# Dense weight loads traced two uses ahead in the second half of a mixer, with the early expert loads queued behind them

## The chip, the cores and the metric

The kernel runs on one core of a Trainium2 chip. The metric is the device time of one execution in microseconds; the runs of the kernel before gave a median of 1898.48 us (1895.02 to 1900.64, three runs).

## The reference, cut to what matters

The network takes 256 tokens of width 1024 through one block of a first kind and two layers of a second kind. Only the second kind matters here. Each of its layers is a mixer followed by a mixture of experts:

```python
proj = jnp.einsum('bsd,dc->bsc', h, w_in)
qa, ka, va, qw, kw, vw, gates = jnp.split(proj, SPLITS, axis=-1)
oa = dilated_mixture(qa, ka, va);  ya = oa @ w_branch_a
ob = banded_attention(qw, kw, vw); yb = ob @ w_branch_b
g = sigmoid(gates + b_gate)
merged = g[:, :, 0] * ya + g[:, :, 1] * yb
x = x + merged @ w_out
...
gate, idx = lax.top_k(softmax(h @ w_router).T, cap)      # 32 tokens for each of 16 experts
ye = (silu(xe @ w_gate) * (xe @ w_up)) @ w_down          # xe = h[idx]
```

All weights are float32. The 16 experts of a layer have 192 MB of weights, the mixer some 32 MB.

## The kernel before, in words

Tokens lie on the free axis and features on the partitions, so a product with a weight matrix is a row of dense tiles. A weight chunk is 128 x 2048 float32, 1 MB, and is called a dense load: `load` (L116) takes a tile of the pool `ring`, which has three slots (`RING`, L54), and issues the DMA on SyncE's queue (L118). `split_w` (L121) then cuts each half of the chunk in a high and a low part, ScalarE writing the high part (L124, a cast) and VectorE the low part (L125, a subtraction). The result `ws` has four slots (`NSPLIT`). `mm3` (L129 to L132) does three matmuls with each 128x128 block. A ring slot is free again when both halves of its chunk are split; a `ws` slot when TensorE has used it, and when a POOL copy that reads it (below) is done.

`mixer` (second layer kind) has two halves. In the first the projections and both attentions are computed. The second begins after `att.close()`, which ends the pool of the attention's tiles: eight gate chunks (`gate(0)` to `gate(3)`, two chunks each, L922), five chunks of the branch matrices `w_br2` (L941), each chunk serving 16 blocks of the loop over `i` and `k`, and four chunks of `w_out2` in `out_tiles` (L684). In the order of use the 17 chunks are: gate 0 to 3, branch 0, branch 1, gate 4, gate 5, branch 2, gate 6, gate 7, branch 3, branch 4, out 0 to 3. Branch 0 ends before the loop's block 16, but the second half of branch 1 is first split after gates 4 and 5. At the end of every `i` a `merge` (L260) follows on VectorE and ScalarE; every gate chunk is followed by `over_rms` (L213, VectorE) and a tanh (L927, ScalarE).

The experts' weights stream through `Experts` (L1008). It has 23 places of 1 MB before any place comes free again: one `q`, four `a0`, six `a1` (in the memory that the attention gives back), `Ha` and `Hb` (the mixer's input, free after gate 7), one `b`, the three ring slots, the four `ws` slots and two more. Loads into `q` and `a0` are made in the mixer's first half. The six into `a1` come from `pace`, which is called after each gate chunk and at each branch chunk and loads one chunk as long as fewer than 11 are there. A paced load first has a one-column copy on GpSimd (L1040), which reads the low part of the newest split (`turn[0]`) and writes the place: so it can't start before that split, and the split's `ws` slot can't be reused before the copy.

The order of instructions on each engine is written by a planner: it simulates the program in time with its own costs, and gives each engine the ready instruction that was traced first. So the gate chunks, which don't need the attention's result, are run between the attention's instructions. On the chip each engine runs its list in order, SyncE's DMA issues too. As far as the trace's semaphores show, a tile gets the slot that comes free first. `tc.issue_after(x)` makes the planner put the DMAs traced in its block behind `x` on the same queue.

Of the kernel before, what the change touches and what calls it, by code (L numbers as in the profile page):

```python
# [53 lines left out]
RING, NA0, NA, NB, NSPLIT = 3, 4, 6, 1, 4  # L54
# [7 lines left out]
def tile_net(ctx: ExitStack, tc: tile.TileContext, a, out):  # L62
    nc = tc.nc
# [4 lines left out]
    sp = ctx.enter_context(tc.tile_pool(name="split", bufs=NSPLIT))  # L68
# [42 lines left out]
        return ps.rearrange("p (n t) -> p n t", n=2)  # L111


    turn = [None]

    def load(src):  # L116
        w = ring.tile([P, CH], F32, name="w", tag="w")
        nc.sync.dma_start(w, src)  # L118
        return w

    def split_w(sp, w, hf):  # L121
        ws = sp.tile([P, 2, 1024], F32R, name="ws", tag="ws")
        s = w[:, hf * 1024 : hf * 1024 + 1024]
        nc.scalar.copy(ws[:, 0], s)  # L124
        nc.vector.tensor_tensor(ws[:, 1], s, ws[:, 0].bitcast(F32), op=ALU.subtract)  # L125
        turn[0] = ws[:, 1]
        return ws[:, 0], ws[:, 1]
# [10 lines left out]
    def dense_pair(ps, w, sp, h, begun=None):  # L138

        for n in range(2):  # L140
            wh, wl = begun if begun and n == 0 else split_w(sp, w, n)
            dense_tile(ps[:, n, :], wh, wl, h)
# [18 lines left out]
    def act_pair():  # L161
        return tuple(hp.tile([P, KT, T], F32R, name=f"H{c}", tag=f"H{c}") for c in "ab")
# [113 lines left out]
    def first_block():  # L276
        with ExitStack() as es:
# [19 lines left out]
            h = act_pair()  # L297
# [223 lines left out]
            with tc.tile_pool(name="b1g", bufs=2, side="right", reuse_waits="tile") as gp:  # L521
# [69 lines left out]
                M = qp.tile([P, 2, KT, T], F32R, name="M", tag="Qa")  # L591
                for i in range(8):
                    w = load(a["w_br"][i])
                    pA, pB = psd(), psd()
                    outs = [pA[:, 0:T]] * 8 + [pA[:, T:]] * 4 + [pB[:, 0:T]] * 4
                    for hf in range(2):
                        wh, wl = split_w(sp, w, hf)
                        for kk in range(8):
                            k = hf * 8 + kk
# [3 lines left out]
                h = act_pair()  # L603
                acc = new_acc()
                for j in range(4):
                    for k, ps in out_tiles(a["w_out1"][j], j, sp, M, psd):
                        nc.vector.tensor_tensor(x[:, k, :], ps, x[:, k, :], op=ALU.add)
                        square_in(acc, x[:, k, :], k == 0)
                        feed(h, k, vec("norm2_g", k))


            with tc.tile_pool(name="b1f", bufs=2) as tp:
# [5 lines left out]
                for j in range(DFF_T):  # L618
                    ps = pairs(psd())
# [12 lines left out]
                h = act_pair()  # L632
# [6 lines left out]
                blk = 0  # L639
                for c in range(11):  # L640
                    w = load(a["w_down1"][c])
                    for hf in range(2):
                        wh, wl = split_w(sp, w, hf)
                        for kk in range(8):
                            n, k = divmod(blk, DFF_T)
                            if k == 0:
                                ps = psd()
# [33 lines left out]

        return h, stats

    def out_tiles(src, j, sp, M, psd):  # L684

        w = load(src)
        for n in range(2):
            ps = psd()
            wh, wl = split_w(sp, w, n)
            dense_tile(ps[:, :T], wh, wl, (M[:, 0], M[:, 1]))  # L690
            yield 2 * j + n, ps[:, :T]


    def mixer(l, h, stats, w0=None):

        with ExitStack() as es:
# [31 lines left out]
            w1 = a["w_in2"]  # L728
# [74 lines left out]
            for j, pair in enumerate(WIN_PAIRS):  # L803
# [30 lines left out]
                for c in range(2):  # L834
                    for t in range(2):
                        i = 2 * c + t
# [26 lines left out]
            for j in range(2):  # L863
                pts = []
                for c in range(2):
                    s = 2 * j + c
                    b = slice(64 * c, 64 * c + 64)
                    pt = tp.tile([P, 2, 4, P], F32, name="pd", tag="zw")
                    pts.append(pt)
                    for t in range(2):  # L870
                        tk = slice(t * P, t * P + P)
                        z = tp.tile([P, 512], F32, name="zd", tag="pt", bufs=3)
                        ps = pss()
                        parts = ((s, slice(0, T), slice(0, T)), (4 + s, slice(256, 384), tk), (8 + s, slice(384, 512), tk))
                        score(ps[:, :T], qa0[:, j, c, tk], ka0[:, j, c], kl0[:, j, c])
                        for n, o, kr in parts[1:]:
                            i = n // 2 - 2
# [35 lines left out]
            M = qp.tile([P, 2, KT, T], F32R, name="M", tag="Qa")  # L913
            blk = 0
            tgs = []

            def gate(j):
                tg = yp.tile([P, 2, 2, T], F32, name="tg", tag="tg", bufs=2)
                tgs.append(tg)
                for i in range(2):  # L920
                    ps = pairs(psd())
                    dense_pair(ps, load(w1[l, 15 + 2 * j + i]), sp, h)  # L922
                    xl.pace()
                    over_rms(tg[:, i], ps, rms)
                    for n in range(2):
                        c = 8 * i + 2 * j + n
                        nc.scalar.activation(  # L927
                            tg[:, i, n, :], tg[:, i, n, :], AF.Tanh, bias=hb[:, c : c + 1], scale=0.5
                        )

            gate(0)
            for i in range(8):
                if i % 2 == 0 and i < 6:
                    gate(i // 2 + 1)
                if i == 5:

                    xl.prefetch(2, True)
                ps = psd()
                for k in range(10):
                    if blk % 16 == 0:  # L940
                        w = load(a["w_br2"][l, blk // 16])  # L941
                        xl.pace()
                    if blk % 8 == 0:
                        wh, wl = split_w(sp, w, blk // 8 % 2)
                    b = blk % 8 * P
                    mm3(ps[:, 0:T] if k < 2 else ps[:, T:], cols(wh, b, P), cols(wl, b, P),
                        Y[:, 0, k, :], Y[:, 1, k, :], k in (0, 2), k in (1, 9))
                    blk += 1
                merge(M, i, [tgs[i // 2][:, b, i % 2, :] for b in range(2)], [ps[:, 0:T], ps[:, T:]])
# [7 lines left out]
            at = PV["router"][0] + 256 * l  # L957
            pl = pss()
            for j in range(4):
                for k, ps in out_tiles(a["w_out2"][l, j], j, sp, M, psd):  # L960
                    gain = vec("norm_ffn", 8 * l + k)
                    if k < KT - 1:
                        nc.vector.tensor_tensor(x[:, k, :], ps, x[:, k, :], op=ALU.add)
                        nc.vector.tensor_scalar(xg[:, k, :], x[:, k, :], gain, None, op0=ALU.mult)
                        square_in(acc, x[:, k, :], k == 0)
                    else:
                        nc.vector.tensor_scalar(xg[:, k, :], x[:, k, :], gain, None, op0=ALU.mult)
                        nc.vector.scalar_tensor_tensor(xg[:, k, :], ps, gain, xg[:, k, :], op0=ALU.mult, op1=ALU.add)
                        nc.vector.tensor_tensor(x[:, k, :], ps, x[:, k, :], op=ALU.add)
                        sq7 = cp.tile([P, T], F32, name="sq7", tag="sq", bufs=2)  # L970
                        nc.scalar.activation(sq7, x[:, k, :], AF.Square)
                if j == 2:

                    nc.scalar.activation(cp.tile([P, 1], F32, name="far1", tag="far1"), acc[:, 0:1], AF.Sqrt)
                if j % 2 == 1:
                    for k in range(2 * j - 2, 2 * j + 2):
                        o = 32 * (k % 4)
                        nc.tensor.matmul(
                            pl[o : o + 32, :T], pv[:, at + 32 * k : at + 32 * k + 32], xg[:, k, :],
                            start=j == 1, stop=j == 3,  # L980
                        )
# [26 lines left out]
    class Experts:  # L1008


        def __init__(self, l):
            self.l, self.r2a, self.r2b, self.at, self.dma = l, [], None, 0, None
            self.have, self.n = [], 0

            self.cycle = ["q"] + ["a0"] * NA0 + ["a1"] * NA + ["Ha", "Hb"] + ["b"] * NB + ["r"] * RING + ["s"] * NSPLIT
            self.places = self.cycle + ["x", "x"]

        def load(self, paced=False):
            i = len(self.have)
            end = i >= NCHUNK - sum(cn for _, cn in ENDS) * KT // 512  # L1020
            while True:
                where = self.places.pop(0)
                if not self.places:
                    self.places = list(self.cycle)

                if not (end and where in ("Ha", "Hb")):
                    break
            if where == "x":
                t = self.extra.pop(0).rearrange("p a d -> p (a d)")
            elif where == "s":  # L1030
                t = sp.tile([P, 2, 1024], F32, name="we", tag="ws").rearrange("p a d -> p (a d)")
            else:
                pool, tag = {
                    "q": (qp, "Qb"), "a0": (self.r2a[0], "w2"), "a1": (self.r2a[-1], "w2"), "b": (self.r2b, "w3"),
                    "r": (ring, "w"), "Ha": (hp, "Ha"), "Hb": (hp, "Hb"),
                }[where]
                t = pool.tile([P, CH], F32, name="we", tag=tag)
            if paced:

                nc.gpsimd.tensor_copy(t[:, 0:1], turn[0][:, 0:1].bitcast(F32))  # L1040
            src = a["w_exp"][self.l, i]

            for c0, cn in ((0, 1024), (1024, 1024)) if i == NCHUNK - 1 else ((0, CH),):
                with tc.issue_after(self.dma.ins) if end else nullcontext():
                    self.dma = nc.sync.dma_start(t[:, c0 : c0 + cn], src[:, c0 : c0 + cn])
            self.have.append(t)

# [3 lines left out]

        def pace(self):

            if len(self.have) < 1 + NA0 + NA:
                self.load(True)

        def take(self):
            while len(self.have) <= self.n:
                self.load()
            self.n += 1  # L1060
            return self.have[self.n - 1]
# [404 lines left out]
```

## Time and profile before

| | |
|---|---|
| median of the runs | 1898.48 us |
| the profiled execution | 1898.55 us, its span 1896.8 us |
| TensorE, matmuls | 1600.4 us busy, 84% of the span |
| VectorE / ScalarE / GpSimd | 43% / 33% / 2% |
| DMA | 562.49 MB, 297 GB/s over the span |
| mean granted clock | 0.888 |

The first block runs from 0 to some 500 us. Then come the first layer's mixer (to 745 us), its router and experts (to some 1190 us), the second layer's mixer (to 1442 us) and its experts. Busy shares over the whole span mix stages with different limits: TensorE is the busy engine in the mixers, and the DMA engines are it in the experts' stages, at some 420 GB/s.

### The profile page before, as it was taken

To read this page: it belongs to the slowest core of one execution; us is meant where nothing else is said; L and a number is where in the kernel's file an instruction comes from. 1 tells how busy PE (TensorE), PEld (TensorE's weight loads), DVE (VectorE), ACT (ScalarE), POOL (GpSimd) and SP (SyncE) were. 2 spreads that over 40 slices of the span, in tenths; PEclk is the share of its full clock that TensorE was granted. 3 is DMA by queue.
4 is the path that set the end of the run, shared out by engine and by line. 5 is a ranking of instruction groups with operands and counts; after the bars stand their busy time and mean duration, and the time that the engine had idled before them with its cause. 6 is when DMAs were issued, how large, how long until landed. Compare 5 with 4: busy or idle time off the path is not lost.

```text
span 1896.8 us, 27588 instructions
## 1 busy us (share of the span) xinstructions
PE 1600.4 (84%) x11434; PEld 1081.8 (57%) x11434; DVE 823.2 (43%) x1481; ACT 629.2 (33%) x1130; POOL 46.3 (2%) x72
## 2 busy tenths in 40 slices
PE   8999999999999988876767666999898866766665
PEld 7899999999998987220111102888896311101101
DVE  7688787996687556100000001687464100000001
ACT  5567646666566443100000001566443100000001
POOL 0100000000011000000000000010000000000000
PEclk9999999999999999887777768999999887867768
DMA  6454554554553367999999999832577999999998
GB/s 248 167 190 167 178 178 179 187 190 178 217 223 112 147 267 275 397 419 420 420 420 419 420 420 418 332 129 102 222 266 277 418 420 419 419 420 419 420 421 321
DMA packets 83829, 562.49 MB, mean 297 GB/s; under 512 B 9452, under 2 KB 14456, under 8 KB 16888
## 3 DMA queue, kind: packets, MB, share of 16 engines
q1 hardware_dynamic: 83544, 560.20, 74.7%
q8 instruction: 90, 1.47, 0.3%
q10 hardware_dynamic: 160, 0.52, 0.1%
q14 instruction: 35, 0.29, 0.0%
HBM read 558.84 MB, written 1.85 MB: 296 GB/s over the span
## 4 chain that ended last, share of the span: by engine, by line
PE 54%; DMA 43%; DVE 2%; ACT 1%; issue 0%; SPq 0%; ACTq 0%; DVEq 0%
DMA we<-in_w_exp_dram 42%; PE ps_d L130 14%; PE ps_d L131 14%; PE ps_d L132 14%; PE ps_t L257 1%; PE ps_g L1172 1%; PE ps_v L846 1%; DMA w<-in_w_in_dram 1%; PE ps_u L1172 1%; PE ps_s L772 1%; PE ps_s L878 1%; PE ps_s L773 0%; PE ps_s L374 0%; PE ps_t L1187 0%; PE ps_v L896 0%
## 5 line engine op out<-in xcount | busy, mean ns | idle before, releaser
L130 PE MATMUL ps_d<-Ha,ws 128*128 128x256 f32 x1408 | 404.9, 288 | 14.7 <-ACT Ha L177 7.9
L132 PE MATMUL ps_d<-Ha,ws 128*128 128x256 f32 x1408 | 404.9, 288 | 5.0 <-DVE ws L125 4.9
L131 PE MATMUL ps_d<-Hb,ws 128*128 128x256 f32 x1408 | 403.6, 287 | 0.7 <-DVE Hb L178 0.7
L125 DVE TENSOR_TENSOR ws<-w,ws 128x1024 fp32r<-128x1024 f32 x282 | 342.6, 1221 | 119.7 <-ACT ws L124 117.0
L124 ACT CAST ws<-w 128x1024 fp32r<-128x1024 f32 x282 | 293.3, 1047 | 256.0 <-PE ps_d L132 223.3
L130 PEld LDWEIGHTS ps_d<-Ha,ws 128*128 128x128 f32 x1408 | 273.0, 194 | 18.4 <-ACT Ha L177 7.9
L132 PEld LDWEIGHTS ps_d<-Ha,ws 128*128 128x128 f32 x1408 | 273.0, 194 | 8.3 <-DVE ws L125 6.1
L131 PEld LDWEIGHTS ps_d<-Hb,ws 128*128 128x128 f32 x1408 | 272.9, 194 | 3.5 <-issue 1.2
L1172 PE MATMUL ps_u<-we,W 128*32 128x512 f32 x992 | 187.8, 836 | 90.4 <-DMA we<-in_w_exp_dram 90.3
L1172 PE MATMUL ps_g<-we,W 128*32 128x512 f32 x1024 | 175.9, 789 | 71.9 <-DMA we<-in_w_exp_dram 71.8
L1172 PE MATMUL ps_e<-we,W 128*32 128x512 f32 (+1 forms) x1152 | 162.6, 669 | 64.2 <-DMA we<-in_w_exp_dram 64.1
L1172 PEld LDWEIGHTS ps_u<-we,W 128*32 128x32 f32 x992 | 25.4, 125 | 239.2 <-DMA we<-in_w_exp_dram 223.1
L1172 PEld LDWEIGHTS ps_g<-we,W 128*32 128x32 f32 x1024 | 26.5, 123 | 205.7 <-DMA we<-in_w_exp_dram 165.3
L1246 ACT ACTIVATE W<-ps_g 128x512 f32<-128x512 f32 x16 | 9.6, 597 | 381.4 <-PE ps_g L1172 381.4
L1172 PEld LDWEIGHTS ps_e<-we,W 128*32 128x32 f32 x1152 | 29.4, 120 | 163.6 <-DMA we<-in_w_exp_dram 121.1
L1248 DVE SCALAR_TENSOR_TENSOR W<-W,ps_u 128x512 f32<-128x512 f32 x16 | 11.0, 688 | 247.1 <-PE ps_u L1172 247.1
L1201 DVE COPY W<-ps_e 128x512 f32<-128x512 f32 (+1 forms) x18 | 11.4, 632 | 221.5 <-PE ps_e L1172 221.5
L1247 DVE SCALAR_TENSOR_TENSOR W<-W,ps_g 128x512 f32<-128x512 f32 x16 | 11.0, 688 | 208.1 <-ACT W L1246 208.1
L1253 ACT COPY W<-ps_t 128x512 f32<-128x512 f32 x16 | 9.4, 586 | 275.9 <-PE ps_t L1252 275.9
L130 PE MATMUL ps_d<-Y,ws 128*128 128x256 f32 x288 | 81.4, 283 | 0.0
L132 PE MATMUL ps_d<-Y,ws 128*128 128x256 f32 x288 | 81.4, 283 | 0.0
L131 PE MATMUL ps_d<-Y,ws 128*128 128x256 f32 x288 | 81.4, 282 | 0.0
(327 smaller groups left out, 2371.9 us busy)
## 6 DMA issues: line engine op xcount, KB each, us to landing
we<-in_w_exp_dram SPq DMA_DIRECT2D x378, 1024.0 KB, 19.9
w<-in_w_in_dram SPq DMA_DIRECT2D x46, 1024.0 KB, 4.9
w<-in_w_up_dram SPq DMA_DIRECT2D x22, 1024.0 KB, 4.8
w<-in_w_br_dram SPq DMA_DIRECT2D x18, 1024.0 KB, 4.9
w<-in_w_gate_dram SPq DMA_DIRECT2D x12, 1024.0 KB, 4.9
w<-in_w_out_dram SPq DMA_DIRECT2D x12, 1024.0 KB, 4.9
w<-in_w_down_dram SPq DMA_DIRECT2D x11, 1024.0 KB, 4.9
w<-in_w_rnn_dram SPq DMA_DIRECT2D x8, 1024.0 KB, 4.8
```

The lines of the kernel that those rows point to most:

```text
L124: nc.scalar.copy(ws[:, 0], s)
L125: nc.vector.tensor_tensor(ws[:, 1], s, ws[:, 0].bitcast(F32), op=ALU.subtract)
L130: nc.tensor.matmul(ps, wh, xh, start=first, stop=False)
L131: nc.tensor.matmul(ps, wh, xl, start=False, stop=False)
L132: nc.tensor.matmul(ps, wl, xh, start=False, stop=last)
L257: nc.tensor.transpose(ps[:, i * P : i * P + P], b, ident)
L772: nc.tensor.matmul(ps, q, kh, start=True, stop=False)
L846: nc.tensor.matmul(po[64 * c : 64 * c + 64, :T], vw[:, k, kvh * 64 : kvh * 64 + 64], pts[c][:, k * T : k * T + T], start=k == 0, stop=k == 1,)
L878: nc.tensor.matmul(ps[:, o], qa[b, i, tk], ka[b, i, kr], start=True, stop=True)
L1172: nc.tensor.matmul(b[32 * e : 32 * e + 32, :cn], lhs[:, k, 32 * e : 32 * e + 32], cols(w, ((k - k0) * 4 + e) * cn, cn), start=k == 0, stop ...
L1201: nc.vector.tensor_copy(ye[:, s], E[:, :cn])
L1247: nc.vector.scalar_tensor_tensor(th, th, 1.0, G[n], op0=ALU.add, op1=ALU.mult)
```

## The change

Three things are changed. `line_up` takes the list of the 17 chunks in the order of use and gives a function `take`; each `take` first traces loads until three are traced and not yet taken, and hands out the oldest. So a load is traced two uses ahead of its own use; before it was traced at its use. `Experts.load` puts each paced load behind `turn[1]`, the dense load that was traced last. And the first four calls of `pace` in a layer load nothing (`self.wait = 4`), so the `a1` loads are traced at branch 0, branch 1, gate 4, gate 5, branch 2 and gate 6; before at gates 0 to 3, branch 0 and branch 1. `out_tiles` gets the tile instead of the source; for the first block this changes nothing.

```diff
     def load(src):
         w = ring.tile([P, CH], F32, name="w", tag="w")
-        nc.sync.dma_start(w, src)
+        turn[1] = nc.sync.dma_start(w, src)
         return w
+    def line_up(srcs):
+        srcs, ws = list(srcs), []
+        def take():
+            while srcs and len(ws) < RING:
+                ws.append(load(srcs.pop(0)))
+            return ws.pop(0)
+        return take
...
-                    dense_pair(ps, load(w1[l, 15 + 2 * j + i]), sp, h)
+                    dense_pair(ps, take(), sp, h)
...
+            order = [w1[l, 15], w1[l, 16]]
+            for i in range(8):
+                if i % 2 == 0 and i < 6:
+                    order += [w1[l, 17 + i], w1[l, 18 + i]]
+                order += [a["w_br2"][l, b // 16] for b in range(10 * i, 10 * i + 10) if b % 16 == 0]
+            take = line_up(order + [a["w_out2"][l, j] for j in range(4)])
...
-                        w = load(a["w_br2"][l, blk // 16])
+                        w = take()
                         xl.pace()
...
-                for k, ps in out_tiles(a["w_out2"][l, j], j, sp, M, psd):
+                for k, ps in out_tiles(take(), j, sp, M, psd):
...
-            self.have, self.n = [], 0
+            self.have, self.n, self.wait = [], 0, 4
...
-                with tc.issue_after(self.dma.ins) if end else nullcontext():
+                behind = self.dma if end else turn[1] if paced else None
+                with tc.issue_after(behind.ins) if behind else nullcontext():
...
         def pace(self):
-            if len(self.have) < 1 + NA0 + NA:
+            self.wait -= 1
+            if self.wait < 0 and len(self.have) < 1 + NA0 + NA:
                 self.load(True)
```

## Rows read from the trace of the kernel before

**Rows 1.** Page, part 4: shares of the chain that ended last, by engine.

```profile
PE 54%; DMA 43%; DVE 2%; ACT 1%; issue 0%; SPq 0%; ACTq 0%; DVEq 0%
```

**Rows 2.** Chain of waits, 655 to 800 us: start us, us, what, xcount.

```profile
744.45 0.83 PE ps_v L987 x6
...
757.59 3.52 PE ps_g L1172 x16
...
783.38 19.87 DMA we<-in_w_exp_dram
```

**Rows 3.** Timeline of PE around its two gaps, first layer [idle before <-releaser].

```profile
669.11 0.38 PE L132 MATMUL ps_d<-Ha,ws 128*128 128x256 f32 x1 [2.20 <-DVE ws L125]
...
677.53 0.39 PE L130 MATMUL ps_d<-Ha,ws 128*128 128x256 f32 x1 [2.66 <-ACT ws L124]
```

**Rows 4.** The same two gaps in the second layer.

```profile
1365.17 0.58 PE L132 MATMUL ps_d<-Ha,ws 128*128 128x256 f32 x1 [2.20 <-DVE ws L125]
1375.06 0.39 PE L130 MATMUL ps_d<-Ha,ws 128*128 128x256 f32 x1 [2.66 <-ACT ws L124]
```

**Rows 5.** Timeline of SP's DMA issues, 640 to 700 us, adjacent ones merged.

```profile
643.16 11.00 SPq L1045 DMA_DIRECT2D we<-in_w_exp_dram  x3
655.74 0.33 SPq L118 DMA_DIRECT2D w<-in_w_in_dram  x1
656.91 1.46 SPq L1045 DMA_DIRECT2D we<-in_w_exp_dram  x2
658.48 0.39 SPq L118 DMA_DIRECT2D w<-in_w_in_dram  x1
...
670.22 0.33 SPq L118 DMA_DIRECT2D w<-in_w_br_dram  x1
```

**Rows 6.** L118's loads, issue to landing: 570 to 625 us, then the one at 658.48.

```profile
DMA to landing us min/median/max: 4.8/4.9/5.0
...
DMA to landing us min/median/max: 13.4/13.4/13.4
```

**Rows 7.** Timeline of DVE, then of ACT, from 663 us.

```profile
666.71 0.42 DVE L265 SCALAR_TENSOR_TENSOR m<-tg,ps_d 128x256 f32<-128x256 f32 x1 [1.41 <-PE ps_d L132]
667.84 2.35 DVE L125 TENSOR_TENSOR ws<-w,ws 128x1024 fp32r<-128x1024 f32 x2
...
664.75 1.98 ACT L124 CAST ws<-w 128x1024 fp32r<-128x1024 f32 x2
675.64 0.91 ACT L927 ACTIVATE tg<-tg,hb 128x256 f32<-128x256 f32 x2 [7.27 <-DVE tg L213]
676.45 2.93 ACT L124 CAST ws<-w 128x1024 fp32r<-128x1024 f32 x3
```

**Rows 8.** Windows: stretch, us, busy us (xcount) by engine, PEclk, DMA share, GB/s.

```profile
679.01:682.42 3.41, 3.41 (x18) 3.41 (x17) 3.13 (x3) 1.42 (x2) 0.00 (x0) 0.50 0.46 108
682.42:685.83 3.41, 3.41 (x31) 3.41 (x29) 0.00 (x0) 0.95 (x1) 0.00 (x0) 1.00 1.02 425
1365.17:1368.50 3.33, 3.33 (x15) 3.33 (x16) 1.42 (x2) 0.00 (x0) 0.00 (x0) 0.50 1.02 406
```

**Rows 9.** Windows of the attention's end, the stretch behind it, and up to the experts.

```profile
620.00:652.50 32.50, 32.50 (x238) 28.26 (x236) 17.91 (x48) 14.71 (x30) 0.18 (x1) 1.00 0.27 98
652.50:666.60 14.10, 14.10 (x119) 14.09 (x119) 7.95 (x11) 8.17 (x12) 3.68 (x5) 1.00 0.87 350
700.00:757.50 57.50, 50.59 (x399) 46.85 (x397) 35.63 (x78) 22.99 (x36) 0.31 (x2) 0.94 0.74 286
```

**Rows 10.** Timeline of POOL, 640 to 654 us: copies before the a1 loads.

```profile
640.57 0.18 POOL L1040 COPY we<-ws 128x1 f32<-128x1 f32 x1 [35.61 <-PE ps_d L132]
653.14 0.30 POOL L1040 COPY we<-ws 128x1 f32<-128x1 f32 x2 [12.39 <-ACT Y L157]
```

**Rows 11.** Waits of SP's queue over the whole span: total us, times, longest us.

```profile
SPq L118 <- DVE ws L125: 414.4, 72, 12.0
```

**Rows 12.** Windows for line L130 alone (one of three dense lines): PE busy (xcount).

```profile
635.64:652.50 16.86, 7.34 (x25) 4.75 (x25) 1.00 0.34 125
```

More of the change, by code (lines that the diff above doesn't have):

```diff
@@ L111, in pairs @@
         return ps.rearrange("p (n t) -> p n t", n=2)
-    turn = [None]
+    turn = [None, None]
     def load(src):
         w = ring.tile([P, CH], F32, name="w", tag="w")
-        nc.sync.dma_start(w, src)
+        turn[1] = nc.sync.dma_start(w, src)
         return w
+    def line_up(srcs):
[5 more added lines that the diff above has]
+        return take
     def split_w(sp, w, hf):
@@ L605, in first_block @@
                 for j in range(4):
-                    for k, ps in out_tiles(a["w_out1"][j], j, sp, M, psd):
+                    for k, ps in out_tiles(load(a["w_out1"][j]), j, sp, M, psd):
                         nc.vector.tensor_tensor(x[:, k, :], ps, x[:, k, :], op=ALU.add)
@@ L682, in first_block, with out_tiles @@
         return h, stats
-    def out_tiles(src, j, sp, M, psd):
-        w = load(src)
+    def out_tiles(w, j, sp, M, psd):
         for n in range(2):
```

## The prediction

> **What bounds the kernel now.** I read four views. The page's chain of what ended last says that TensorE (54%) and DMA (43%) set the end, and nothing else does [rows 1]. In order of time the chain is TensorE up to the end of the mixer (744.45) and the router, the experts' first matmuls at 757.59, and from 783.38 one expert load after the other [rows 2]. So a mixer is bound by TensorE and an experts' stage by its stream, which can't run ahead: all 23 places are taken before the experts begin, and the next load waits for a place that they free. What the second half of a mixer gains or loses therefore moves everything behind it by as much, in both layers.
>
> Inside that half the reader is to see that TensorE is busy without a break, 32.50 of 32.50 us and 14.10 of 14.10 us [rows 9], except for two gaps: 2.20 us before 669.11 and 2.66 us before 677.53 [rows 3], and the same two, to the hundredth, in the second layer [rows 4]. The first ends with a subtraction of `split_w` on VectorE, the second with one of its casts on ScalarE.
>
> Where they come from is read from SyncE's queue. Three `a1` loads are issued from 643.16 on, then gate 4's chunk at 655.74, two more `a1` loads, gate 5's chunk at 658.48, and branch 2 only at 670.22 [rows 5]. A dense load that has the queue to itself lands 4.9 us after issue; gate 5's took 13.4 us, so it landed at 671.9 [rows 6]. Gate 4's first cast is at 664.75 [rows 7], 9.0 us after its issue, though ScalarE had been free. Late data then meets lists in a fixed order: gate 4's subtraction stands behind the merge that ends branch 0 and 1, which waits for TensorE until 666.71, and gate 5's cast stands behind gate 4's tanh at 675.64, whose input TensorE has only just finished [rows 7]. I take it that the planner wrote these orders because in its own timeline, too, the chunks came late.
>
> **The change part by part.** No matmul, cast, subtraction or byte is added or removed; only DMA issues and copies on GpSimd move.
>
> *The queue's order.* The `a1` loads now stand behind, in turn, gate 4, gate 5, branch 2, gate 6, gate 7 and branch 3. Gate 4's chunk can't be issued before 655.74, for it waits for a ring slot; what it loses is the two megabytes issued just ahead of it. It lands at 655.74 + 4.9 = 660.6, about 4 us sooner than its cast shows now. Gate 5 at 658.48 then has at most one `a1` load ahead, 1.05 MB at 420 GB/s = 2.5 us (425 and 406 in [rows 8]), so it lands between 663.4 and 665.9, 6 us sooner or more.
>
> *First gap.* TensorE wants gate 4's low part at 666.9. A cast of about 1 us and a subtraction of 1.2 us (two take 1.98 and 2.35 [rows 7]) after 660.6 are done by 663 to 664, before the merge's first instruction at 666.71. So the 2.20 us go. *Second gap.* TensorE leaves gate 4 at 674.9 now, at 672.7 then, and gate 5's chunk has been there for 7 us or more, ahead of the tanh. So the 2.66 us go. Next late would be branch 2: its slot comes free with gate 4's splits, by 665 instead of 670.22, so it lands by some 673 with one `a1` load ahead of it. TensorE comes to it after gate 5 (48 matmuls at 0.12 us, 5.8 us) and 12 blocks (36, 4.3 us), at 672.7 + 10.1 = 683: slack enough. Two mixers: 2 x (2.20 + 2.66) = 9.7 us.
>
> *The clock.* The granted clock is 1.00 up to 666.60 [rows 9] and falls to 0.50, the 1.2 GHz level, for one stretch of 3.41 us at 679.01, behind the two gaps; in the second layer once behind each gap, at 1365 and at 1375 us. The stretches at 679.01 and 1365.17 start 18 and 15 matmuls, where one at 1.00 starts 31 in 3.41 us [rows 8]; the third, whose row isn't shown, starts 18 as the first does. The loss is 13/31 x 3.41 = 1.4 us, (30.3 - 15)/31 x 3.41 = 1.7 us and 1.4 us, 4.5 us together. With no gap ahead nothing in these rows asks for a fall, so I take the whole 4.5; the bounds are 0 and 4.5.
>
> *The six `a1` loads, later.* They are issued between some 656 and 685 instead of 643 to 660. They must be there when the experts begin, at 757.5. Even if all six slipped past 700, the DMA engines are 0.74 busy from there on and have 0.26 x 57.5 = 15 us free for their 6 x 2.5 = 15 us [rows 9]. Cost: 0; upper bound one load's 2.5 us in a mixer, if it lands just ahead of an `out` chunk with no slack.
>
> *The copies and the skipped paces.* In the first layer's trace the copy for gate 0's split is made at 640.57, those for gates 1 and 2 at 653.14 [rows 10], when the attention gives its memory back: until then the undone copies hold up to two of the four `ws` slots. The change drops these copies, so gates 2 and 3 can be split earlier, between the attention's instructions. TensorE has no idle time there that this could fill [rows 9], so I cost it at 0. What it may cost is the slower rival below. The copies that remain come behind splits whose place is free, 0.2 us each on an engine that is 2% busy: 0.
>
> *Lookahead by itself.* The ring keeps its three slots, and the loads already go out when a slot comes free. Tracing them earlier gives nothing more: 0.
>
> The sum, against the profiled execution (1898.55 us; its span 1896.80; the median of the runs, 1898.48, is the same within 0.1 us): 1898.55 - 9.7 - 4.5 = **1884.3 us**.
>
> **A rule that speaks against it.** Two gaps of one size that repeat in both layers look like a regular shortage. The Trainium skill (Perfetto Trace Analysis, Optimization Strategy) says that consistent bubbles on the engine that should be saturated can mean there isn't room for the next tile to be allocated. By that rule the ring would have to grow and this change, which leaves it at three slots, would give nothing: 1898.5 us. The trace agrees in part: SyncE's queue waits 414.4 us in all for splits that free a ring slot [rows 11]. But gate 5's 13.4 us come after its issue, where no slot is missing any more.
>
> **The rivals.** *A: nothing moves (1898.5, from 1896 to 1901).* The slots bind: gate 4 can't be issued earlier, and the planner keeps merge before subtraction and tanh before cast, since it counts with its own costs. For it speak [rows 11]; against it, that these orders only make sense for late data.
>
> *B: one gap goes (about 1892).* Subtraction and cast stand on different engines and are ordered each by itself. Without the first gap: 2 x 2.20 and one clock stretch of 1.6 give 1892.5; without the second: 2 x 2.66 and 1.6 give 1891.6. For it speaks that the queue's order helps gate 5 more (13.4 us) than gate 4 (9.0).
>
> *C: slower, the attention's cover is spent early (about 1902).* From 635.64 to 652.50 the attention's last softmax chains run on VectorE and ScalarE, and TensorE is kept busy by 3 x 25 dense matmuls of gates 2 and 3 (L130; the other two lines alike [rows 12]), 75 x 0.12 = 9.0 us at the spacing of [rows 9] (14.10 us for 119). With the `ws` slots free, the planner may run these matmuls before 635; then the tail is bare and TensorE waits up to 9.0 us in each mixer. 1898.55 - 14.2 + 2 x 9.0 = 1902.3. It turns the sign once more than 7.1 us of cover are lost in a mixer. For it: the copies do hold the slots [rows 10]. Against it: the planner gives the attention's instructions precedence, and gates 4 and 5, whose ring slots then also come free sooner, can cover the tail as well.
>
> *D: the queue stalls.* SyncE's list is in order; an `a1` load behind a dense load whose slot isn't free waits with it, and the dense loads behind both. Branch 2 is the tight one, traced before branch 1's second split. Price: up to 2.5 us per mixer in place of one gap, so about 1889.
>
> **How the numbers follow.** Forecast 0.57 (own range 1880 to 1888), D 0.07, B 0.11, A 0.12, C 0.13. A measurement of this kernel can tell some 0.3%, 5.7 us, from no change, so faster means below 1892.8. Forecast, D and, as it lies on the edge, a third of B are there: 0.67. A, the rest of B and a small part of C make 0.21 for the same, C's rest 0.12 for slower. The range of 8 in 10 takes in the forecast, D, B and A's faster part, and leaves out C and the odd low case: 1879 to 1899.
>
> **What would show it.** Right: in both layers no TensorE gap over 1 us between 600 and 745 us, gate 4's and gate 5's loads landing within 8 us of issue with no expert load issued between 640 and 655, the granted clock 1.00 through that stretch, and the experts' stage as long as now from its first matmul on. Wrong: gaps before the same lines (A, B), dense matmuls gone from the stretch before the attention's last products and a gap there (C), or expert loads still in flight when the experts begin, so that their stage is longer.

## The result, and the profile after

The changed kernel takes 1885.38 us (median of four, 1882.87 to 1886.21) against 1898.9 us in the runs beside it: a ratio of 0.9929, 95% interval 0.9911 to 0.9947. That is 13.5 us less, and 1.1 us above the forecast of 1884.3. The profiled execution's span is 1883.3 us against 1896.8.

The first view is TensorE's waits in the first layer's mixer, where [rows 3] showed the two gaps (who waited for whom, total us, times, longest us):

```profile
PE ps_v L213 <- DVE rtok L681: 2.7, 1, 2.7
PE ps_o L1109 <- DVE lg L1106: 0.3, 1, 0.3
```

The first of these is in the mixer's first half and was there before; the second is the router. Nothing is left of the two gaps, and in the second layer's mixer [rows 4] the same view is empty. The stretch from the attention's last product to the mixer's last matmul, in both layers, is the measure from here on (columns as in [rows 8]). In the kernel before:

```profile
652.58:743.02 90.44, 85.58 (x693) 83.41 (x695) 55.23 (x87) 40.11 (x57) 3.98 (x7) 0.98 0.74 285
1348.65:1440.57 91.92, 87.06 (x692) 84.89 (x695) 55.44 (x87) 40.02 (x57) 3.98 (x7) 0.96 0.74 280
```

In the changed kernel:

```profile
653.96:737.55 83.59, 83.59 (x692) 81.82 (x695) 53.52 (x85) 38.13 (x55) 1.50 (x7) 1.00 0.77 296
1341.72:1425.32 83.60, 83.60 (x693) 81.83 (x695) 53.64 (x85) 38.07 (x55) 1.50 (x7) 1.00 0.78 296
```

The reader is to see the same number of matmuls, TensorE busy for the whole of the stretch, and the granted clock at 1.00. Both stretches are 83.6 us now; they were 90.4 and 91.9. So 6.85 and 8.32 us are gone, 15.2 us in all. The span gained 13.5, so 1.7 us net are given back outside the stretches: 1.4 us in the first layer's mixer ahead of the stretch (last section) and 1.8 us in the second layer's experts, which take 443.1 us from their first matmul to the end instead of 441.3, less 1.5 us gained between the first layer's experts' start and the second stretch. The 1.8 us are not shown to be a price of the change: in skip_two (below), whose stretches are as short, that stage takes 441.7 us.

SyncE's issues, which answer to [rows 5] (L118 is a dense load, L1062 an expert load):

```profile
646.85 0.33 SPq L118 DMA_DIRECT2D w<-in_w_in_dram  x1
647.23 0.42 SPq L1062 DMA_DIRECT2D we<-in_w_exp_dram  x1
657.59 0.33 SPq L118 DMA_DIRECT2D w<-in_w_in_dram  x1
658.26 0.55 SPq L1062 DMA_DIRECT2D we<-in_w_exp_dram  x1
666.47 0.33 SPq L118 DMA_DIRECT2D w<-in_w_br_dram  x1
666.85 0.42 SPq L1062 DMA_DIRECT2D we<-in_w_exp_dram  x1
673.36 0.33 SPq L118 DMA_DIRECT2D w<-in_w_in_dram  x1
```

Dense and expert loads alternate. Gate 4's chunk goes out at 646.85, nine microseconds sooner than in [rows 5], gate 5's at 657.59. The time from issue to landing of these two, which answers to [rows 6], is:

```profile
DMA to landing us min/median/max: 4.8/4.8/4.8
...
DMA to landing us min/median/max: 5.2/5.2/5.2
```

And GpSimd's copies, which answer to [rows 10]:

```profile
646.94 0.18 POOL L1056 COPY we<-ws 128x1 f32<-128x1 f32 x1 [40.60 <-PE ps_t L268]
658.05 0.19 POOL L1056 COPY we<-ws 128x1 f32<-128x1 f32 x1 [10.92 <-DVE ws L136]
```

The reader is to see two copies at different times, where [rows 10] has two that waited together for the attention's end. The splits that they read end at 646.82 and 657.57, so each copy comes within half a microsecond of its split (the long idle time in brackets is GpSimd's, which had nothing else to do), and no split slot is held until the attention ends at 653.96.

### The profile page after: what moved, and what is told of

Same layout as the page of the kernel before. It is cut to its first block, busy times and chain, and to the rows that moved or that the text cites. A ratio compares the mean times of both kernels' runs of the same rounds, so it can differ in the third digit from the quotient of the medians.

```text
span 1883.3 us, 27589 instructions
## 1 busy us (share of the span) xinstructions
PE 1594.7 (85%) x11434; PEld 1076.1 (57%) x11434; DVE 825.0 (44%) x1481; ACT 628.9 (33%) x1130; POOL 41.2 (2%) x72
## 4 chain that ended last, share of the span: by engine, by line
PE 53%; DMA 44%; DVE 1%; ACT 1%; issue 0%; SPq 0%; POOL 0%; ACTq 0%
DMA we<-in_w_exp_dram 42%; PE ps_d L141 14%; PE ps_d L142 14%; PE ps_d L143 14%; PE ps_t L268 2%; PE ps_v L856 1%; PE ps_g L1190 1%; DMA w<-in_w_in_dram 1%; PE ps_u L1190 1%; PE ps_s L782 1%; PE ps_s L888 1%; PE ps_s L783 1%; PE ps_t L1205 0%; PE ps_s L385 0%; PE ps_v L906 0%; PE ps_v L912 0%
```

## The experiments

Two things had to be told apart: which of the three parts of the change does it, and by what. *Theory 1* is the prediction's: expert loads ahead of gates 4 and 5 make their chunks late. *Theory 2* says that the copies that wait for the attention's memory hold split slots, so the splits, the ring slots and the next loads come late.

**skip_alone** and **no_skip** try the parts by themselves. skip_alone has the skipped paces only; no_skip has the lookahead and the demanded order, but skips no pace.

```diff
 skip_alone, against the kernel before:
-            self.have, self.n = [], 0
+            self.have, self.n, self.wait = [], 0, 4
...
+            self.wait -= 1
-            if len(self.have) < 1 + NA0 + NA:
+            if self.wait < 0 and len(self.have) < 1 + NA0 + NA:
 no_skip, against the changed kernel:
-            self.have, self.n, self.wait = [], 0, 4
+            self.have, self.n, self.wait = [], 0, 0
```

> The kernel before with one part of the change alone: the first four paces of a layer load nothing. No lookahead, no order between expert loads and dense loads. The prediction put the gain down to the order of the queue that is demanded of the planner: by that account this kernel keeps both gaps in each mixer, 1898 us. Rival: the skipped paces do it all, since a load that is traced after gate 3 has nothing to be put ahead of: both gaps gone, 1885 us, the same queue as in the changed kernel.

> The changed kernel with all paces loading again: lookahead and the demanded order stay. By the prediction's account the order alone takes the gaps away: about 1885 us. Rival (the skipped paces do it all): the a1 loads are traced at gates 0 to 3 and branches 0 and 1 again, the demanded order then only names dense loads that are issued long before, so the queue is that of the kernel before: both gaps, 1898 us.

skip_alone takes 1885.32 us, ratio 0.9913 (0.9898 to 0.9927), and TensorE has no gap in the second half of either mixer. Its two stretches are those of the changed kernel:

```profile
655.00:738.60 83.60, 83.60 (x693) 81.83 (x695) 53.50 (x85) 38.15 (x55) 1.49 (x7) 1.00 0.78 296
1342.32:1425.92 83.60, 83.60 (x693) 81.83 (x695) 53.64 (x85) 38.07 (x55) 1.49 (x7) 1.00 0.77 296
```

no_skip takes 1899.89 us, ratio 0.9994 (0.9984 to 1.0004), with the old gaps. These are its TensorE waits in the second layer's mixer:

```profile
PE ps_d L141 <- ACT ws L135: 2.7, 1, 2.7
PE ps_d L143 <- DVE ws L136: 2.2, 1, 2.2
```

So the skipped paces are the whole of the change. The traces agree: on VectorE, ScalarE, GpSimd and SyncE skip_alone's instructions run in the order of the changed kernel's, and no_skip's in that of the kernel before. So neither the demanded order nor the lookahead changed what the planner writes. With three ring slots the lookahead can't load earlier than a slot comes free. Why the skipped paces put gate 4's load first is argued and not shown: I take it that what matters is the split that a paced load's copy waits for. It is gate 3's or a later one now, where it was gate 0's, and a load that waits for gate 3's can't go out before the ring slot of the same split comes free for gate 4.

**held_behind** and **free_ahead** have each theory's cause without the other's. held_behind claims the places and makes the copies at the first six paces, but fetches later (`held` is the list of places that wait for their load). free_ahead holds no slot, since its copy is a memset that reads no split, but puts the six expert loads first.

```diff
 held_behind, against the changed kernel:
-            if self.wait < 0 and len(self.have) < 1 + NA0 + NA:
-                self.load(True)
+            if len(self.have) < 1 + NA0 + NA:
+                self.load(True, later=True)               # place and copy, no DMA
+            if self.wait < 0 and self.held:
+                self.fetch(*self.held.pop(0), True)       # the DMA, behind turn[1]
...
 free_ahead, against the kernel before:
-                nc.gpsimd.tensor_copy(t[:, 0:1], turn[0][:, 0:1].bitcast(F32))
+                if 1 + NA0 <= i < 1 + NA0 + NA:
+                    nc.gpsimd.memset(t[:, 0:1], 0.0)
+                else:
+                    nc.gpsimd.tensor_copy(t[:, 0:1], turn[0][:, 0:1].bitcast(F32))
...
-                    dense_pair(ps, load(w1[l, 15 + 2 * j + i]), sp, h)
+                    with tc.issue_after(xl.dmas[1 + NA0 + 2 + 2 * i].ins) if j == 2 else nullcontext():
+                        w = load(w1[l, 15 + 2 * j + i])
+                    dense_pair(ps, w, sp, h)
```

> The changed kernel, but the six a1 places are claimed and copied into at the first six paces as before, so that the copies hold split slots until the attention gives its memory back; only the loads themselves come where the change puts them, behind the dense loads. Theory 1 (late data: expert loads ahead of gates 4 and 5 in the queue): gate 4's chunk is issued at about 655.7 as before and lands within 6 us, no TensorE gap over 1 us, 1885 us. Theory 2 (held split slots delay the splits, and with them the ring slots and the next loads): gate 4's chunk is still issued at 655.7, 9 us later than in the changed kernel, both gaps stay, 1897 to 1899 us.

> The kernel before, but the copy ahead of each a1 load is a one-column memset that reads no split, so that no split slot is held, and gate 4's chunk is put behind the third a1 load, gate 5's behind the fifth. All six a1 loads stand ahead of both chunks. Theory 1 (late data): gate 4's chunk is issued from 653 on and lands 13 us or more later, with six megabytes at 2.5 us ahead of it, gaps of 2 us or more in each mixer, 1896 to 1906 us. Theory 2 (held split slots): the slots are free, gaps gone, 1885 us.

held_behind takes 1884.61 us, ratio 0.9916 (0.9901 to 0.9931). Its copies wait as in the kernel before:

```profile
641.98 0.18 POOL L1056 COPY we<-ws 128x1 f32<-128x1 f32 x1 [35.62 <-PE ps_d L143]
654.55 0.30 POOL L1056 COPY we<-ws 128x1 f32<-128x1 f32 x2 [12.38 <-ACT Y L168]
```

Gate 4's chunk goes out as late as before, at 657.15, but with no expert load just ahead of it:

```profile
644.20 0.33 SPq L118 DMA_DIRECT2D w<-in_w_br_dram  x1
657.15 0.33 SPq L118 DMA_DIRECT2D w<-in_w_in_dram  x1
657.53 1.25 SPq L1070 DMA_DIRECT2D we<-in_w_exp_dram  x1
659.42 0.33 SPq L118 DMA_DIRECT2D w<-in_w_in_dram  x1
```

It lands 5.6 us after that, and both stretches are as short as in the changed kernel:

```profile
654.00:737.57 83.57, 83.57 (x692) 81.80 (x695) 55.30 (x87) 39.82 (x57) 3.98 (x7) 1.00 0.84 321
1341.47:1425.04 83.57, 83.57 (x692) 81.80 (x695) 55.36 (x87) 39.92 (x57) 3.98 (x7) 1.00 0.84 322
```

free_ahead takes 1903.7 us, ratio 1.0013 (1.0004 to 1.0022). The first fence shows its queue, the second TensorE's gap (the second layer's is 6.12 us):

```profile
640.70 15.22 SPq L1050 DMA_DIRECT2D we<-in_w_exp_dram  x6
656.02 0.93 SPq L118 DMA_DIRECT2D w<-in_w_in_dram  x2
```

```profile
673.06 0.58 PE L130 MATMUL ps_d<-Ha,ws 128*128 128x256 f32 x1 [6.37 <-ACT ws L124]
```

Gate 4's chunk lands 15.8 us after its issue, at 671.9; the cast (1 us) and the matmul at 673.06 follow at once. Theory 2 is out: the kernel with slots held and loads behind is fast, the one with slots free and loads ahead is slow.

**free_order** asks whether each gap belongs to one chunk. It is free_ahead without the demanded order of gates 4 and 5 (the second part of its diff is left out).

> As free_ahead (a memset in place of the copy, so no split slot is held), but without the demanded order: the queue then has gate 4's chunk first, all six a1 loads after it, and gate 5's chunk behind them. If each gap belongs to one late chunk: gate 4's chunk is issued before 650 and lands in 5 us, the first gap is gone; gate 5's chunk has six loads of 2.5 us ahead of it, issued from 653 on, so it lands at about 671 as in the kernel before and the second gap stays in both mixers: 1890 to 1894 us. Rival (one early chunk gives the lists enough slack for both): no gap, 1885 us.

It takes 1890.93 us, ratio 0.9952 (0.9939 to 0.9964). These are its queue and TensorE's waits:

```profile
646.65 0.33 SPq L118 DMA_DIRECT2D w<-in_w_in_dram  x1
647.03 10.16 SPq L1048 DMA_DIRECT2D we<-in_w_exp_dram  x6
657.39 0.33 SPq L118 DMA_DIRECT2D w<-in_w_in_dram  x1
```

```profile
PE ps_d L130 <- ACT ws L124: 2.7, 1, 2.7
```

Gate 4's chunk is early and the first gap is gone; gate 5's lands 15.7 us after its issue and the second gap is there, in both layers. So each gap goes with its own chunk.

**list_only** asks whether it is the late data or the list. It has the queue, paces and copies of the kernel before; only gate 5's first cast and subtraction stand ahead of gate 4's scaling and tanh (`laid` holds the newest cast and the newest subtraction).

```diff
...
+                    if j == 2 and i == 0:
+                        w = load(w1[l, 20])
+                        begun = split_w(sp, w, 0)
+                    with tc.issue_after(laid[1].ins) if j == 2 and i == 0 else nullcontext():
                         over_rms(tg[:, i], ps, rms)
...
+                        with tc.issue_after(laid[0].ins) if j == 2 and i == 0 else nullcontext():
                             nc.scalar.activation(...)      # the tanh
```

> The kernel before, with only the order of instructions on ScalarE and VectorE changed at gates 4 and 5: gate 5's first cast and subtraction are put ahead of gate 4's scaling and tanh. DMA queue, paces and copies as before. Gate 5's chunk lands at about 671.9, TensorE leaves gate 4 at 674.9. If the second gap is late data meeting a fixed list, and the list is half of it: the cast is done by 673 and the second gap (2.66 us) goes in both mixers, the first (2.20 us) stays; with one or two clock stretches less about 1890 to 1894 us. Rival: the data alone is too late whatever the list says: a gap of the same size at the same place, 1899 us.

It takes 1891.47 us, ratio 0.9957 (0.9941 to 0.9972). The second gap is gone in both layers, the first stays:

```profile
670.53 0.39 PE L133 MATMUL ps_d<-Ha,ws 128*128 128x256 f32 x1 [2.20 <-DVE ws L126]
```

On ScalarE gate 5's cast now waits for the data alone, which still lands 13.4 us after its issue, and is done ahead of TensorE's need:

```profile
673.43 1.04 ACT L125 CAST ws<-w 128x1024 fp32r<-128x1024 f32 x1 [3.64 <-DMA w<-in_w_in_dram]
```

So the second gap was no shortage of data on the chip: the chunk lands as late as before, in time, and the list kept it waiting. In the changed kernel the planner itself puts this cast (666.81) ahead of gate 4's tanh (674.88). That it orders so by when the chunk lands in its own timeline fits both lists, but is argued. In free_ahead, with six loads ahead, the data really is late.

**ring4** and **ring4_ahead** test the rule of the missing slot: both have a fourth ring slot and one `a0` place less.

```diff
 both:
-RING, NA0, NA, NB, NSPLIT = 3, 4, 6, 1, 4
+RING, NA0, NA, NB, NSPLIT = 4, 3, 6, 1, 4
...
             parts_q(qa0, load(w1[l, 6]))
-            xl.prefetch(1, True)
 ring4_ahead besides: gate 4's load behind the third a1 load, gate 5's behind the fifth, as in free_ahead
```

> The kernel before with four ring slots for dense loads instead of three, and three a0 places instead of four (23 places in all as before, one expert load less in the first half of the mixer). A test of the rule that consistent bubbles mean missing slots. Gate 4's chunk then finds a slot before the attention ends and is issued ahead of the a1 loads. Slots rule: both gaps go, 1885 us. Late data: the same for gate 4, since it is early; gate 5's chunk stands behind three a1 loads, lands some 7 us late and may still be in time: no gap or the second one alone, 1885 to 1893 us.

> As ring4, but gate 4's chunk is put behind the third a1 load and gate 5's behind the fifth, as they stand in the kernel before. Slots rule: four slots, so the gaps stay away, 1885 us. Late data: the queue is that of the kernel before, so both gaps are back whatever the slots, 1896 to 1902 us.

ring4 takes 1883.97 us, ratio 0.992 (0.9903 to 0.9937), with no gap: gate 4's chunk finds a slot at 642.96 and goes out ahead of the expert loads. ring4_ahead takes 1898.61 us, ratio 0.9996 (0.9986 to 1.0007), with both gaps in both layers (the first layer's are shown):

```profile
PE ps_d L130 <- ACT ws L124: 2.7, 1, 2.7
PE ps_d L132 <- DVE ws L125: 2.2, 1, 2.2
```

Another slot is a second way to be early in the queue; by itself it gives nothing.

**skip_two** has `self.wait = 2` in the changed kernel, so two paces are skipped instead of four.

> The changed kernel with two skipped paces instead of four. Its queue has gate 4's chunk ahead of all a1 loads, and three a1 loads between gate 4's and gate 5's. Late data: gate 4 in time; gate 5's chunk lands after gate 4's own and up to three megabytes (7.5 us), some 12 us after issue at the worst, and TensorE wants it 5.8 us after gate 4's start at about 667: with an issue at 658 it lands by 670, in time for the cast. No gap, 1885 us. If each expert load ahead of gate 5 counts by itself: the second gap is back, about 1892 us.

It takes 1884.6 us, ratio 0.9922 (0.9905 to 0.9939), and has no gap. Three expert loads stand between gates 4 and 5, gate 5's chunk lands 8.3 us after its issue at 657.70, and that is soon enough. Neither ring4 nor skip_two is told apart from the changed kernel by these intervals; all have TensorE without a gap in this stretch, so there is no more to gain here by loading sooner.

## Why the prediction was right, and where it was not

*Both gaps go, 9.7 us:* right, to the hundredth in both layers, and for the reason given: the chunks of gates 4 and 5 behind expert loads. held_behind and free_ahead show it, free_order gap by gap.

*"The queue's order":* the step failed in what it credits. It made the demanded order (`turn[1]`) the cause and costed "the copies and the skipped paces" at 0. The order on the queue is what counts, but it is the skipped paces that make it: skip_alone, without the demanded order, gains all of it (1885.32 us), and no_skip, with it, has both gaps (1899.89 us). The 0 for the lookahead was right.

*"Gate 4's chunk can't be issued before 655.74":* wrong. It goes out at 646.85, since no copy holds a split slot and gate 3 is split sooner; in free_order, where no slot is held either, it goes out at 646.65. That wasn't needed: held_behind, with the slots held, issues at 657.15 and is as fast. One of the signs named for being right therefore did not come: an expert load is issued between 640 and 655, at 647.23, but behind gate 4's chunk.

*The fixed lists:* right for the second gap, as list_only shows. For the first, whose subtraction stands behind a merge, it is argued, not tried by itself. [rows 7] speaks for it: gate 4's first cast is done by 665.8, VectorE then waits for TensorE until 666.71, and a subtraction of 1.2 us right behind the cast would have ended at some 667.0 (an estimate), where TensorE stops at 666.9.

*The clock, 4.5 us:* right in kind, a little small: the granted clock is 1.00 in both stretches, as forecast. The stretches shrink by 6.85 - 4.86 = 2.0 and 8.32 - 4.86 = 3.5 us beyond the gaps, 5.5 in all. list_only gives the price of one fall by itself:

```profile
654.00:741.53 87.53, 85.33 (x693) 83.36 (x695) 55.15 (x87) 39.92 (x57) 3.98 (x7) 0.98 0.77 294
1345.12:1431.17 86.05, 83.85 (x693) 81.88 (x695) 55.35 (x87) 39.85 (x57) 3.98 (x7) 1.00 0.78 300
```

Both stretches have the 2.20 us gap; the first has one fall besides and is 1.5 us longer. Against held_behind's 83.57 us it is 2.20 + 1.76 us longer.

*The six loads later, at 0:* right; in the first layer the experts begin 14.5 us after the mixer's last matmul in both kernels (752.06 - 737.55, and 757.52 - 743.02), and from there to the second mixer's first matmul it is 433.1 us, before 433.7.

*Rival C, the attention's cover,* did not come. There is no gap at the attention's end, although the ring slot of gate 3 comes free 9 us sooner there. *D, the stalled queue,* did not come either: branch 2 goes out at 666.47, sooner than the 670.22 of [rows 5]. *A, the slots rule,* did not come. The gaps repeated, but ring4_ahead has the room and keeps them. The Trainium skill (Perfetto Trace Analysis, Optimization Strategy) says that consistent bubbles can mean that there isn't room for the next tile; here the trace differs.

That the sum came within 1.1 us is in part luck. It had 1.0 us too little for the clock and lacked the 1.7 us given back elsewhere, and these two partly cancel; the other 0.4 us is that the kernel before ran at 1898.9 us beside the changed one, where the sum starts from 1898.55.

## What to carry to other kernels

When a stage bound by TensorE has short gaps behind a split or a cast, compare issue to landing of the load behind it with one that has the queue to itself: a load that nobody needs yet, issued just ahead, can delay it by its whole length (in free_ahead gates 4's and 5's chunks, of 1 MB each, are issued 0.5 us apart and land 2.5 us apart). By way of the fixed lists the engine can then wait even where the data lands in time, as list_only shows; where there is slack, as in skip_two, it loses nothing. Trace a background load after the urgent ones that become ready at the same moment, and tie it to work that comes late enough. Try the parts of a change one by one: here one of the three did all of it.

## What the runs showed of the hardware that was not expected

The granted clock does not fall after every gap of one size. In the kernel before, TensorE waited 2.66 us ahead of 510.02, in the first half of the mixer, and kept a clock of 1.00. In the changed kernel the same wait, ahead of 509.88, is followed by a fall to 0.50. The first row is of the kernel before, the second of the changed one (columns as in [rows 8]):

```profile
510.71:514.12 3.41, 3.41 (x31) 3.41 (x30) 2.95 (x7) 2.96 (x7) 0.18 (x1) 1.00 0.94 356
510.71:514.12 3.41, 3.41 (x18) 3.41 (x18) 3.08 (x8) 2.96 (x6) 0.18 (x1) 0.50 0.98 351
```

With it the attention ends at 653.96 instead of 652.58, which are the 1.4 us given back there. This is not shown to come of the change: all eleven traces of this case have that wait, and seven show a fall behind it, among them free_order and list_only, which are edits of the kernel before and hold no part of the change. In list_only the same 2.20 us gap is followed by a fall in the first layer and by none in the second, whose stretch is then 86.05 us, 0.3 above 83.57 + 2.20. So a gap of this length costs itself for certain, and some 1.5 to 1.8 us more only at times.
